# Four small moves in the queue order of an encoder-layer kernel: last dilated merge, dilated transposes, local output, q,k squares

## The chip, the cores and the metric

The kernel runs on one core of one Trainium2 chip. The metric is the device time of one execution in microseconds. Three runs of the kernel before gave 1829.3, 1828.5 and 1827.25 us, median 1828.5.

## What is computed

One encoder layer on x of 1024 tokens by 1024 features, float32:

```
x += 1/2 * post(SwiGLU_1(pre(x)))
qkv = pre(x) @ w_qkv                       # 16 heads of 64
o_na  = neighbourhood_attention(heads 0-7)     # 16 x 64 token grid, window 8 x 16, learned bias
o_dil = softmax-weighted mixture over (window, dilation) in (128,1), (512,4), (2048,16), heads 8-15
x += post(concat(rmsnorm(o_na), rmsnorm(o_dil)) @ w_out)
x += 1/2 * post(SwiGLU_2(pre(x)))
```

Each `pre` and `post` is an RMS norm with a gain. For the dilated heads each pattern gives an output and a log-sum; the outputs are merged with the softmax of the log-sums.

## The kernel before, in words

**Matmuls.** Products are made in float32r with two parts for each operand: a high part (a cast, on ScalarE) and a low part (the operand minus its high part, on VectorE), and three matmuls high*high, high*low, low*high. A 128x512 block of output is one PSUM bank. The large products (feed-forward, q,k,v) use seven-product block schemes; the output projection is plain.

**Order.** The program is written out by hand for TensorE: within the `ordered()` blocks its instructions run as written. The other engines' queues are put in order by the framework's scheduler, from the written order and its own idea of when an operation is ready, except where `c.behind(f, engine...)` ties all that f issues behind the last instruction written so far for that engine. Two queues of small work are carried along with the matmuls. `c.todo` holds turns: one entry is taken at each `c.tick()`. `c.steps` and `c.sums` hold smaller pieces: `c.step()` takes one of each. `plan(n, {turn: [...]})` fills `c.todo`, after first running everything that is left.

**Value and q,k start.** `Passes.run(0, 1)` for the value projection has 12 turns, of one `c.step()` each for the first eight and two for the last four. During them the last four 128-token tiles of x are finished: `Finish.rest(ts, h)` puts on `c.sums` two additions (L892), then `Operand.norm` (L218): the squares on ScalarE (L166), tied behind what was written last for ScalarE, after which the root (`rstd_of`, L147 to L159, a chain of twelve or thirteen small VectorE operations) and the scaling of the tiles (L230) follow as further entries. `A(4, 5)` and `A(6, 7)` are such calls for tiles 4, 5 and 6, 7; their x is loaded before. `U(4)` puts tile 4's transposes (L174) on `c.steps`, and `pg.split_left(0)` makes the parts of the first q,k weights (L462, L463), tied behind VectorE's and ScalarE's last. Then `pg.ahead` starts q,k: matmuls at L472, L473 (high part of the weight) and L478 (low part). `pg.save` copies an accumulator out (L488) before more is added to it.

**Attention.** Heads 8 to 15 (dilated) come first, then heads 0 to 7 (neighbourhood). A unit is one pair of score blocks: scores into PSUM (L1192, L1325), bias and maximum on VectorE (L1095), exponential on ScalarE (L1097), and, three units later, transposes on TensorE (L1105), the copy of them (L1107, by turns on VectorE and ScalarE), and one unit later the product with v (L1225, L1341). Every second unit ends with `c.tick()`, so a turn is two units. For each pair of dilated heads one pattern's outputs go through HBM to be regrouped (L1251 is the load back), and `DilPair.merge` makes the weights: small VectorE operations L1261 to L1271 with one exponential between (L1264), then two products on GpSimd (L1281, L1282) and the addition on VectorE (L1285). Merge, products, nothing, addition take a turn each. Only the last pair (head pair 7) has `self.then`, which is `attended()`: it queues the norm of the dilated outputs, first four turns of squares (L1370), the root and the first scaling, an empty turn, four turns with transposes, casts and low parts (`GroupNorm.put`, L174, L181), then `begin`, which makes the 16 fillers (the output projection's matmuls that only need the first half of the dilated rows), then the second half in the same way. Fillers are placed between later units at a rate of 16 / (units left + 2); what is left over comes behind the last unit.

**Local output.** After the last unit, TensorE runs the first half of a product that needs only dilated rows into four held banks (L363 to L365), and between its matmuls it transposes the eight 128-token blocks of the local heads' output (`GroupNorm.put` with `strip`, L1401; two PSUM buffers, so a block waits for the block before the last to be read). Each block has two halves, each a cast (L1405) and a low part (L1406). The first four blocks share one root and the last four another (`early[1].scale`, root and two scalings, L1390); the latter's own squares of the last head are made on VectorE (L1378).

Of the kernel before, what the change touches and what calls it, by code (L numbers as in the profile page):

```python
# [10 lines left out]
F32 = mybir.dt.float32  # L11
# [5 lines left out]
SP, POOL, DVE, ACT = [getattr(mybir.EngineType, e) for e in ("SP", "Pool", "DVE", "Activation")]  # L17
# [160 lines left out]
def transpose_in(c, x, hi, lo):  # L178

    ps = transposed(c, x)  # L180
    c.nc.scalar.copy(hi, ps)  # L181
    c.nc.vector.tensor_sub(lo, ps, hi.bitcast(F32))  # L182
    return ps


class Operand:
# [58 lines left out]
    def put(self, t):  # L245

        for i in range(2):
            self.c.steps.append(lambda: self.one(t))
# [862 lines left out]
class DilPair:  # L1111
# [97 lines left out]
    def outs(self, hd, part, quad, un, pt, po):  # L1209
        c, nc = self.c, self.c.nc  # L1210
        if un == 0:
            po.append(c.pso.tile([P, 4, P], F32, tag="o", name="po"))
        po, f = po[0], slice(hd * 64, hd * 64 + 64)
        if (part, quad, un) == (0, 1, 0):
            nc.tensor.matmul(po[:, 0:4:3, f], pt[:, 1, :], self.va[:, 8:10, f], start=True, stop=False,
                             skip_group_check=True)
            for j in range(2):
                nc.tensor.matmul(po[:, 3 * j, f], pt[:, 2 * j, :], self.va[:, 7 + 3 * j, f], start=False, stop=True,
                                 skip_group_check=True)
        else:  # L1220
            for j, blk in enumerate(self.blocks(part, quad, un)):
                o = 1 + j if quad and not part else un * 2 + j
                for t in range(2):
                    rhs = self.vb[:, blk // 2, t, :] if part else self.va[:, blk - 1 + t, :]
                    nc.tensor.matmul(po[:, o], pt[:, 2 * j + t, :], rhs, start=t == 0, stop=t == 1)  # L1225
        if un == 0:
            return
        to = self.oa.rearrange("p (a b) w -> p a b w", a=2)[:, :, 0:4:3, f] if quad else (
            self.oa.rearrange("p (a b) w -> p a b w", a=2)[:, :, 1:3, f])
        got = po[:, :, f]  # L1230
        if part:
            to = self.ob.rearrange("p (j c) w -> p c j w", j=2)[:, 2 * quad:2 * quad + 2, :, f]
            got = got.rearrange("p (c j) w -> p c j w", j=2)
        else:
            got = got.rearrange("p (a b) w -> p a b w", a=2)
        (nc.scalar.copy if quad else nc.vector.tensor_copy)(to, got)
        if hd and part:
            self.regroup(quad)
        c.tick()
        if (hd, part, quad) == (1, 0, 1):  # L1240
            c.todo.extend([lambda: None] + [lambda: c.behind(self.merge, DVE, ACT)])

    def regroup(self, quad):

# [10 lines left out]
    def merge(self):  # L1255

        c, nc, sa, obn = self.c, self.c.nc, self.sa, self.obn
        w = c.op.tile([P, 2, 8, 2], F32, tag="w", name="w")
        mn = c.op.tile([P, 8, 2], F32, tag="mn", name="mn")
        na, nb = sa[:, :, 0:2], obn[:, :, P:P + 2]  # L1260
        nc.vector.tensor_tensor(mn, na, nb, op=ALU.min)  # L1261
        nc.vector.tensor_sub(w[:, 0], mn, na)
        nc.vector.tensor_sub(w[:, 1], mn, nb)
        nc.scalar.activation(w, w, AF.Exp)  # L1264
        dn = c.op.tile([P, 2, 8, 2], F32, tag="dn", name="dn")
        nc.vector.tensor_mul(dn[:, 0], w[:, 0], sa[:, :, 2:4])
        nc.vector.tensor_mul(dn[:, 1], w[:, 1], obn[:, :, P + 2:P + 4])
        nc.vector.tensor_add(dn[:, 0], dn[:, 0], dn[:, 1])
        nc.vector.reciprocal(dn[:, 0], dn[:, 0])
        nc.vector.tensor_mul(w[:, 0], w[:, 0], dn[:, 0])  # L1270
        nc.vector.tensor_mul(w[:, 1], w[:, 1], dn[:, 0])  # L1271

        def bc(i):
            return w[:, i].unsqueeze(3).broadcast_to([P, 8, 2, 64])

        def hv(a):
            return a.rearrange("p b (h f) -> p b h f", h=2)
        a4, b4 = hv(self.oa), hv(obn[:, :, 0:P])

        def products():  # L1280
            nc.gpsimd.tensor_mul(b4, b4, bc(1))  # L1281
            nc.gpsimd.tensor_mul(a4, a4, bc(0))  # L1282

        def add():
            nc.vector.tensor_add(hv(c.og[1][:, :, self.pi * P:(self.pi + 1) * P]), a4, b4)  # L1285
        c.todo.extendleft(([self.then] if self.then else []) + [lambda: c.behind(add, DVE), lambda: None,
                          lambda: c.behind(products, POOL)] + ([] if self.then else [lambda: None]))


def na_v(c, p):  # L1290
# [65 lines left out]
class GroupNorm:  # L1356
# [35 lines left out]
    def put(self, i):  # L1392
        c, nc, b, ot = self.c, self.c.nc, self.b0 + i, self.ot
        o = self.og[:, b, :]
        if not self.strip:
            hi, lo = [ot[b // 4][:, j, :, b % 4 * P:b % 4 * P + P] for j in range(2)]
            transpose_in(c, o, hi, lo)
            return
        ps = c.pst.tile([P, 4, P], F32, tag="tr", name="trp")
        for j in range(4):  # L1400
            nc.tensor.transpose(ps[:, j, :], o[:, j * P:(j + 1) * P], c.ident)  # L1401
        for hf in range(2):
            src = ps[:, :, hf * 64:hf * 64 + 64].rearrange("p k (r c) -> p k r c", r=8)
            hi, lo = [ot[hf][:, j].rearrange("p k (r s c) -> p k r s c", r=8, s=8)[:, :, :, b, :] for j in range(2)]
            nc.scalar.copy(hi, src)  # L1405
            nc.vector.tensor_sub(lo, src, hi.bitcast(F32))  # L1406


def layer(tc, a, out):
    nc = tc.nc  # L1410
    c = Ctx(tc)
    with ExitStack() as ctx:
# [51 lines left out]
        def plan(n, at):  # L1464

            c.flush()

            def turn(fs):
                return lambda: [f() for f in fs]
            c.todo.extend(turn(at.get(i, ())) for i in range(n))  # L1470
# [146 lines left out]
        def queued(f):  # L1617

            c.behind(f, SP, POOL)
# [6 lines left out]
        with ExitStack() as order:  # L1626
# [140 lines left out]
            A = lambda *ts: lambda: fin.rest(ts, hs.get)  # L1767

            def vearly(p, t, ps):
# [4 lines left out]
                else:  # L1774
# [3 lines left out]
            pg = PairGemm(c, op, [(a["wqk"][p], a["wqk"][8 + p]) for p in QK_ORDER], 8, QKPairs(c))  # L1778
# [2 lines left out]
            vp.fetch([[w1[:, 0:2], w1[:, 2:4]]])  # L1781
            op.tied = True
            plan(12, {0: [lambda: fin.scale(4, 4), A(4, 5)], 8: [op.second, lambda: c.steps.append(lambda: None), U(4), lambda: queued(pg.start)],
                      9: [lambda: c.behind(lambda: pg.split_left(0), DVE, ACT)], 10: [A(6, 7)]})
            vp.run(0, 1, upto=1)
            e.close()
            early_pools(e, 2, 2)
# [74 lines left out]
        def attended():  # L1862

            ops.close()
            c.xt = pool("xt2", 1, s1)
            xo["part"] = pool("hs0", 1, s1).tile([P, 4, D], F32, name="hs")
            ot = xo["dil"] = [c.xt.tile([P, 2, 4, T], F32R, tag=f"o{h}", name=f"o{h}") for h in range(2)]
            norms = [GroupNorm(c, og[1], b, xo["gd"][:, 512:], False, ot, False) for b in (0, 4)]
            puts = [lambda i=i, n=n: (i < 3 and n.scaled(i + 1), n.put(i)) for n in norms for i in range(4)]
            squares = [lambda i=i: c.behind(lambda: norms[1].squares(slice(0, 512), 0, (i, i + 1)), ACT) for i in (0, 2)]  # L1870
            single = [lambda i=i: c.behind(lambda: norms[0].squares(slice(0, 512), 0, (i,)), ACT) for i in range(4)]
            scales = [lambda n=n: c.behind(lambda: n.scale(1), DVE) for n in norms]

            def begin():
                xo["ws"] = nat_fillers(c, ot[0], xo["part"], (1, 0))
                c.rate = len(c.fillers) / (c.left + 2)
            c.todo.extend(single + [scales[0], lambda: None] + puts[:4] + [begin] + squares + [scales[1], lambda: None])
            c.todo.extend(puts[4:])

        def last(quad):  # L1880
# [6 lines left out]
        early = []  # L1887
# [8 lines left out]
        with ordered():  # L1896
# [31 lines left out]
            puts = deque()  # L1928
            for quad, n in enumerate(early):
                n.ot = on  # L1930
                for i in range(4):
                    if quad and i < 2:
                        puts.append(lambda i=i, n=n: (c.behind(lambda: n.scaled(i + 2), DVE), n.put(i)))
                    elif not quad and i == 0:
                        puts.append(lambda n=n: (n.put(0), c.behind(lambda: early[1].scale(2), DVE)))
                    else:
                        puts.append(lambda i=i, n=n: n.put(i))
        s5.close()
# [3 lines left out]
        with ordered():  # L1942
# [18 lines left out]
            pg = gate_pairs(3, op, a["wg2"], a["wu2"], 11)  # L1961
# [3 lines left out]
            A = lambda *ts: lambda: fin.rest(ts, lambda t: hs[t // 4][:, t % 4, :])  # L1965
# [90 lines left out]
```

## Time and profile before

| | us |
|---|---|
| median of three runs | 1828.5 |
| the profiled execution | 1826.53 |
| its span, first to last instruction | 1824.7 |
| TensorE busy | 1807.9 |
| VectorE busy | 1308.9 |
| ScalarE busy | 831.6 |
| GpSimd busy | 348.8 |

The granted TensorE clock was 0.999 over the span. In rows of the timeline the columns are the start in us from the span's start, the duration in us, the engine (PE TensorE, DVE VectorE, ACT ScalarE, POOL GpSimd, SP SyncE), the source line where the view has one, the operation, the output and input tiles with their shapes, and in brackets the idle time of that engine before it with what ended it. "L" and a number is a line of the kernel before.

### The profile page before, as it was taken

To read this page: it belongs to the slowest core of one execution; us is meant where nothing else is said; L and a number is where in the kernel's file an instruction comes from. 1 tells how busy PE (TensorE), PEld (TensorE's weight loads), DVE (VectorE), ACT (ScalarE), POOL (GpSimd) and SP (SyncE) were. 2 spreads that over 40 slices of the span, in tenths; PEclk is the share of its full clock that TensorE was granted. 3 is DMA by queue.
4 is the path that set the end of the run, shared out by engine and by line. 5 is a ranking of instruction groups with operands and counts; after the bars stand their busy time and mean duration, and the time that the engine had idled before them with its cause. 6 is when DMAs were issued, how large, how long until landed. Compare 5 with 4: busy or idle time off the path is not lost. (4 is left out here: it accounts for less than half of the span.)

```text
span 1824.7 us, 25161 instructions
## 1 busy us (share of the span) xinstructions
PE 1807.9 (99%) x8876; PEld 1521.7 (83%) x8876; DVE 1308.9 (72%) x2225; ACT 831.6 (46%) x1495; POOL 348.8 (19%) x579
## 2 busy tenths in 40 slices
PE   8999999999999999999999999999999999999998
PEld 6888888888888888888999998887888888888886
DVE  6888877776466877577676856778877777664557
ACT  7522233334534556234688765554223333354433
POOL 2124421112021123232344100221111111110000
PEclk9999999999999999999999999999999999999999
DMA  8756566557888867768687523594655566596564
GB/s 295 258 170 220 171 230 224 193 209 268 307 305 294 288 206 266 261 230 292 193 271 255 183 88 116 193 312 159 197 180 194 201 220 224 184 351 198 191 229 146
DMA packets 172769, 409.28 MB, mean 224 GB/s; under 512 B 20401, under 2 KB 42321, under 8 KB 170594
## 3 DMA queue, kind: packets, MB, share of 16 engines
q1 hardware_dynamic: 125168, 248.68, 41.5%
q0 software_dynamic: 46608, 157.41, 23.7%
q8 instruction: 70, 1.15, 0.3%
q10 hardware_dynamic: 866, 1.58, 0.2%
q14 instruction: 57, 0.47, 0.1%
HBM read 280.09 MB, written 132.56 MB: 226 GB/s over the span
## 5 line engine op out<-in xcount | busy, mean ns | idle before, releaser
L472 PE MATMUL mmp<-x,whi 128*128 128x512 f32 (+1 forms) x1464 | 571.7, 391 | 1.1 <-ACT x L181 0.7
L473 PE MATMUL mmp<-x,whi 128*128 128x512 f32 (+1 forms) x1464 | 569.1, 389 | 0.7 <-DVE x L182 0.7
L793 PE MATMUL accp<-pw 128*128 128x512 f32 x1800 | 411.1, 390 | 0.0
L793 PEld LDWEIGHTS accp<-pw 128*128 128x128 f32 x1800 | 337.2, 188 | 70.0 <-ACT hb L814 0.3
L478 PE MATMUL mmp<-x,wlo 128*128 128x512 f32 (+1 forms) x1464 | 390.5, 388 | 0.2 <-DVE wlo L463 0.2
L472 PEld LDWEIGHTS mmp<-x,whi 128*128 128x128 f32 x1464 | 275.7, 188 | 58.7 <-ACT s L488 1.4
L473 PEld LDWEIGHTS mmp<-x,whi 128*128 128x128 f32 x1464 | 275.7, 188 | 57.2 <-DVE x L182 1.4
L478 PEld LDWEIGHTS mmp<-x,wlo 128*128 128x128 f32 x1464 | 274.4, 188 | 57.4 <-DVE wlo L463 0.6
L761 DVE TENSOR_TENSOR pw<-praw,pw 128x1024 fp32r<-128x1024 f32 (+1 forms) x181 | 200.1, 1143 | 125.6 <-ACT pw L760 124.8
L760 ACT CAST pw<-praw 128x1024 fp32r<-128x1024 f32 (+1 forms) x181 | 168.7, 983 | 207.7 <-PE accp L793 167.3
L462 ACT CAST whi<-wraw 128x1024 fp32r<-128x1024 f32 x126 | 132.6, 1053 | 187.4 <-PE mmp L473 157.9
L463 DVE TENSOR_TENSOR wlo<-wraw,whi 128x1024 fp32r<-128x1024 f32 x126 | 153.9, 1222 | 2.9 <-ACT whi L462 2.9
L703 POOL DMA_DIRECT2D g<-sg x44 | 23.9, 544 | 427.6 <-DVE sg L696 246.5
L462 ACT CAST whi<-traw 128x512 fp32r<-128x512 f32 x52 | 32.3, 621 | 122.6 <-DVE traw L564 89.7
L488 ACT COPY s<-mmp 128x512 f32<-128x512 f32 x49 | 28.8, 588 | 127.7 <-PE mmp L478 121.1
L655 DVE TENSOR_TENSOR c<-mmp,u 128x512 f32<-128x512 f32 x52 | 35.9, 691 | 70.9 <-PE mmp L478 70.7
L563 DVE TENSOR_TENSOR wraw<-wraw 128x1024 f32<-128x1024 f32 x52 | 63.6, 1224 | 17.7 <-DMA wraw<-in_wu_dram 17.0
L793 PE MATMUL accp<-pw,x 128*128 128x512 f32 x312 | 71.8, 390 | 0.0
L1095 DVE CUSTOM_DVE_ANT_0 s<-sp,g 128x256 f32<-128x256 f32 (+1 forms) x128 | 48.4, 413 | 30.7 <-PE sp L1192 24.6
L793 PEld LDWEIGHTS accp<-pw,x 128*128 128x128 f32 x312 | 58.3, 188 | 12.4 <-DVE pw L761 0.3
L642 DVE TENSOR_TENSOR c<-mmp,v 128x512 f32<-128x512 f32 x52 | 35.8, 689 | 34.0 <-PE mmp L478 34.0
L1341 PE MATMUL po<-vs,pt 128*128 128x128 f32 x352 | 49.9, 276 | 0.4 <-DVE pt L1107 0.4
(281 smaller groups left out, 2485.7 us busy)
## 6 DMA issues: line engine op xcount, KB each, us to landing
praw<-g SPq DMA_DIRECT2D x70, 512.0 KB
wraw<-in_wg_dram SPq DMA_DIRECT2D x44, 512.0 KB
wraw<-in_wu_dram SPq DMA_DIRECT2D x44, 512.0 KB
tr<-in_wd_dram SPq DMA_DIRECT2D x44, 512.0 KB
g<-sg POOLq DMA_DIRECT2D x88, 256.0 KB, 5.4
ts<-tr POOLq DMA_DIRECT2D x22, 1024.0 KB, 4.7
praw<-ts SPq DMA_DIRECT2D x88, 256.0 KB
praw<-in_wd_dram SPq DMA_DIRECT2D x66, 256.0 KB
```

The lines of the kernel that those rows point to most:

```text
L462: nc.scalar.copy(hi, raw)
L463: nc.vector.tensor_sub(lo, raw, hi.bitcast(F32))
L472: mm(out, hi[:, i, sl], xhi[:, k, cols], start=not go_on and k == 0, stop=False, skip_group_check=go_on)
L473: mm(out, hi[:, i, sl], xlo[:, k, cols], start=False, stop=False, skip_group_check=go_on)
L478: mm(out, lo[:, i, sl], xhi[:, k, cols], start=False, stop=k == 3, skip_group_check=go_on)
L563: nc.vector.tensor_sub(r[:, 0:2], r[:, 1:3], r[:, 0:2])
L655: c.behind(lambda: nc.vector.tensor_add(c21, d, u2), *((DVE,) if self.sink.soon and b == self.n - 1 else ()))
L760: nc.scalar.copy(hi, raw[:, :m])
L761: nc.vector.tensor_sub(lo, raw[:, :m], hi.bitcast(F32))
L793: c.nc.tensor.matmul(acc[t], a, b, start=not chained and gi == 0 and j == i == 0, stop=end and j + n >= len(ops) and i == len(two) - 1, sk ...
L1095: c.nc.vector.tensor_tensor_reduce(out=s, in0=ps, in1=bias, scale=-1.0, scalar=3e38, op0=ALU.add, op1=ALU.min, accum_out=neg)
L1341: nc.tensor.matmul(po[0][:, u], pt[0][:, j, :], vs[:, k0 + j, :], start=j == 0, stop=j == n - 1)
```

## The change

No operation is added or removed. Five places change the order in which work is queued:

- The merge of the last pair gets a second empty turn ahead of it. `self.then` is called in the turn of the addition, no longer in a turn of its own; for the other pairs nothing changes.
- In `attended()` a second empty turn stands between the first root and the first transposes of the dilated rows; all that follows there moves a turn later.
- In `GroupNorm.put` with `strip`, both casts are issued ahead of both low parts.
- The second root of the local output (with its first two scalings) is queued behind the last VectorE instruction before the first block, no longer behind the first block's low parts.
- `A(6, 7)` moves from turn 10 to turn 7 of the 12.

```diff
-            c.todo.extend([lambda: None] + [lambda: c.behind(self.merge, DVE, ACT)])
+            c.todo.extend([lambda: None] * (2 if self.then else 1) + [lambda: c.behind(self.merge, DVE, ACT)])
...
-        c.todo.extendleft(([self.then] if self.then else []) + [lambda: c.behind(add, DVE), lambda: None,
-                          lambda: c.behind(products, POOL)] + ([] if self.then else [lambda: None]))
+
+        def added():
+            c.behind(add, DVE)
+            if self.then:
+                self.then()
+        c.todo.extendleft([added, lambda: None, lambda: c.behind(products, POOL)] +
+                          ([] if self.then else [lambda: None]))
...
+        lows = []
         for hf in range(2):
...
             nc.scalar.copy(hi, src)
-            nc.vector.tensor_sub(lo, src, hi.bitcast(F32))
+            lows.append((lo, src, hi.bitcast(F32)))
+        for args in lows:
+            nc.vector.tensor_sub(*args)
...
-                      9: [lambda: c.behind(lambda: pg.split_left(0), DVE, ACT)], 10: [A(6, 7)]})
+                      9: [lambda: c.behind(lambda: pg.split_left(0), DVE, ACT)], 7: [A(6, 7)]})
...
-            c.todo.extend(single + [scales[0], lambda: None] + puts[:4] + [begin] + squares + [scales[1], lambda: None])
+            c.todo.extend(single + [scales[0], lambda: None, lambda: None] + puts[:4] + [begin] + squares + [scales[1], lambda: None])
...
-                        puts.append(lambda n=n: (n.put(0), c.behind(lambda: early[1].scale(2), DVE)))
+                        puts.append(lambda n=n: (c.behind(lambda: early[1].scale(2), DVE), n.put(0)))
```

## Prediction

> **What bounds the kernel now.** I read the page first, then the busy time of each engine in the three stretches that the change touches, then the timelines of TensorE, VectorE and ScalarE around every gap there.
>
> ```profile
> span 1824.7 us, 25161 instructions
> ...
> PE 1807.9 (99%) x8876; PEld 1521.7 (83%) x8876; DVE 1308.9 (72%) x2225; ACT 831.6 (46%) x1495; POOL 348.8 (19%) x579
> ```
>
> TensorE is busy for 99% of the span, so an edit that adds and removes no matmul can win only what TensorE waits. The next rows give, for the q,k start, the last dilated merge and the local output, the length, then the busy time of PE, PEld, DVE, ACT and POOL with instruction counts, the granted clock, the DMA share and the GB/s.
>
> ```profile
> 655.00:690.00 35.00, 34.88 (x162) 28.59 (x161) 30.86 (x67) 23.67 (x40) 11.72 (x21) 1.00 0.77 257
> 1003.00:1040.00 37.00, 36.19 (x294) 34.71 (x294) 29.57 (x110) 27.18 (x83) 5.40 (x5) 1.00 0.47 164
> 1095.00:1126.00 31.00, 30.40 (x180) 25.58 (x180) 22.31 (x74) 16.48 (x52) 2.37 (x5) 1.00 0.15 46
> ```
>
> Here TensorE idles 35.00 - 34.88 = 0.12, 37.00 - 36.19 = 0.81 and 31.00 - 30.40 = 0.60 us, 1.53 us in all. That is too low a cap, because a matmul counts as busy until its modelled end, after the next one could have begun. The loss is better read from the starts: how much later the next matmul starts than after the same work without a wait. VectorE is busy for 30.86 of 35 us at the q,k start; that matters below.
>
> **The last merge, one turn later.** A turn is two attention units. The first operation of the merge stands in VectorE's queue before the regrouped outputs have landed, and a softmax is queued behind it:
>
> ```profile
> 1009.48 0.18 DVE L1261 TENSOR_TENSOR mn<-sa,obn 128x16 f32<-128x16 f32 x1 [0.95 <-DMA obn<-rg]
> ```
>
> TensorE then waits for a transposed probability tile that VectorE copies too late:
>
> ```profile
> 1010.85 0.38 PE L1105 MATMUL ptp<-ident,pb 128*128 128x128 f32 x2
> 1011.63 0.94 PE L1341 MATMUL po<-vs,pt 128*128 128x128 f32 x6 [0.40 <-DVE pt L1107]
> 1012.32 0.60 PE L1325 MATMUL sp<-st 128*128 128x384 f32 x2
> 1012.76 0.38 PE L1105 MATMUL ptp<-ident,pb 128*128 128x128 f32 x2
> 1012.98 0.61 PE L1341 MATMUL po<-vs,pt 128*128 128x128 f32 x4
> ```
>
> From two transposes to the next product it is 11.63 - 10.85 = 0.78 us here and 12.98 - 12.76 = 0.22 us a unit later: 0.56 us lost. From 10.85 to 12.76 one unit takes 1.91 us, 1.35 without the loss, so a turn is 2.7 us. That covers the 0.95 us wait for the DMA by 1.7 us. The merge's ten small operations come as before, and the 1.55 us that they and the wait cost together (0.95 and about 0.6 of small operations ahead of the late copy) made 0.56 us of loss, so the pipeline absorbs about 1.0; the 0.6 alone are hidden. Gain 0.56 us; if the landing were as late again, nothing.
>
> The rest of the merge moves with it, except the call that begins the norm: it now comes in the turn of the addition instead of one turn later, so its squares stay where they were.
>
> ```profile
> 1012.66 1.90 POOL L1282 TENSOR_TENSOR oa<-oa,w 128x1024 f32<-128x1024 f32 x1 [16.05 <-DVE w L1271]
> 1014.53 1.90 POOL L1281 TENSOR_TENSOR obn<-obn,w 128x1024 f32<-128x1024 f32 x1
> ```
>
> ```profile
> 1016.46 1.23 DVE L1285 TENSOR_TENSOR og<-oa,obn 128x1024 f32<-128x1024 f32 x1 [0.30 <-POOL obn L1281]
> ```
>
> The merge's first operation could have issued at 9.48 - 0.95 = 8.53; a turn later is 11.2, or 1.8 us after its present place. The two products follow and would end at about 1016.4 + 1.8 = 1018.2. The addition's place, 16.46 - 0.30 - 0.56 + 2.7 = 1018.3, is just behind it: a wait of 0 to 0.5 us on VectorE, of the size of the 0.30 that costs nothing now. I take 0. The squares would wait on ScalarE only if the addition ended after their turn, two turns behind the old addition (16.16 - 0.56 + 5.4 = 1021.0); it ends at 1018.3 + 1.23 = 1019.5, so 1.5 us cover it.
>
> **The dilated transposes, one turn later.** The chain of small operations for the root of the norm is interleaved with softmaxes and ends late:
>
> ```profile
> 1035.51 0.83 PE L1341 MATMUL po<-vs,pt 128*128 128x128 f32 x6
> 1036.77 0.63 PE L174 MATMUL trp<-ident,og 128*128 128x128 f32 x4 [0.42 <-DVE og L1390]
> ```
>
> Six products and their follower are 1.26 us apart here and 12.32 - 11.63 = 0.69 us above: 0.57 us lost. With 2.7 us more the rows are scaled long before, so 0.57 us is gained. What moves along are four transposes, their casts and low parts, the first filler of the output product, the second half's squares and scaling. The 16 fillers stay the same matmuls, but are paced over 26 instead of 28 counted units (0.615 instead of 0.571 a unit): TensorE's sum is the same, and a denser filler gives VectorE more time per unit. The turns end before the last head's first turn, so nothing runs out: 0, at worst one more wait of the size seen here, 0.5 us.
>
> **Local output: casts ahead of low parts.** Each transposed block has two halves; ScalarE casts a half, VectorE subtracts it from the same PSUM tile.
>
> ```profile
> 1111.25 0.37 ACT L1405 CAST n<-trp 128x256 fp32r<-128x256 f32 x1 [3.32 <-PE trp L1401]
> 1112.85 0.65 ACT L1405 CAST n<-trp 128x256 fp32r<-128x256 f32 x2 [1.23 <-DVE n L1406]
> ```
>
> ```profile
> 1112.40 0.42 DVE L1406 TENSOR_TENSOR n<-trp,n 128x256 fp32r<-128x256 f32 x1
> 1113.25 0.42 DVE L1406 TENSOR_TENSOR n<-trp,n 128x256 fp32r<-128x256 f32 x1 [0.44 <-ACT n L1405]
> 1113.60 0.15 DVE L147 TENSOR_TENSOR v<-gss 128x4 f32<-128x4 f32 x1
> ```
>
> ```profile
> 1113.12 0.39 PE L364 MATMUL accp<-wlo,o 128*128 128x512 f32 x1
> 1113.34 0.40 PE L365 MATMUL accp<-whi,o 128*128 128x512 f32 x1
> 1113.82 0.63 PE L1401 MATMUL trp<-ident,og 128*128 128x128 f32 x4
> ```
>
> The second cast starts at 1112.85, when the first low part has ended (1112.40 + 0.42), though it doesn't read its result. So the first block gives its buffer back at 1113.67, and the third block's transposes, which take that buffer, start 0.48 us after the matmul before instead of 0.22 to 0.23: 0.25 us lost. With both casts first, they run at 1111.25 and about 1111.6, the low parts follow back to back at 1112.40 and 1112.75, and the buffer is free at 1113.17, 0.4 us ahead of TensorE's 1113.57. Gain 0.25 us, at least 0.
>
> [...]
>
> **Local output: second root sooner.** The second half's root stands behind the first block's low parts, from 1113.60, and its scaled rows come late for the fifth block:
>
> ```profile
> 1117.31 1.42 DVE L1390 SCALAR_TENSOR_TENSOR og<-og,y,gd 128x512 f32<-128x512 f32 x2
> ```
>
> ```profile
> 1117.39 0.39 PE L365 MATMUL accp<-whi,o 128*128 128x512 f32 x1
> 1118.21 0.63 PE L1401 MATMUL trp<-ident,og 128*128 128x128 f32 x4 [0.43 <-DVE og L1390]
> ```
>
> 0.82 instead of 0.23 us: 0.59 lost. The root needs 17.31 - 13.60 = 3.71 us with the low parts that slip in between. Queued before the first block it can start at about 1112.5, behind the last local squares. The first scaled row is then there at 1112.5 + 3.71 + 0.75 = 1117.0, TensorE at 1117.39 + 0.23 - 0.25 = 1117.37. Gain 0.59 us with 0.4 to spare; one more low part in the chain (0.42) and little of the spare is left, so 0.2 to 0.59.
>
> **Squares of q,k's last two tiles.** Their additions, squares and root are queued three turns sooner, before the fifth tile's transposes and the first weights' split instead of after all of it. No load moves, since both tiles are already on the chip. Now the squares hold up ScalarE (two of 1.06 us, the second here), behind them the copy that releases the first q,k accumulator:
>
> ```profile
> 681.62 1.06 ACT L166 ACTIVATE junk<-x 128x1024 bf16<-128x1024 f32 x1
> ```
>
> ```profile
> 683.14 0.59 ACT L488 COPY s<-mmp 128x512 f32<-128x512 f32 x1
> ```
>
> ```profile
> 680.77 0.60 PE L174 MATMUL trp<-ident,x 128*128 128x128 f32 x4
> 681.12 0.48 PE L472 MATMUL mmp<-x,whi 128*128 128x512 f32 x1
> ...
> 682.14 1.08 PE L478 MATMUL mmp<-x,wlo 128*128 128x512 f32 x4
> 683.06 0.60 PE L174 MATMUL trp<-ident,x 128*128 128x128 f32 x4
> 683.78 0.50 PE L472 MATMUL mmp<-x,whi 128*128 128x512 f32 x1
> ```
>
> The matmul at 683.78 starts as that copy ends (683.73), 0.72 us after the transposes, against 0.35 at 680.77: 0.37 lost, and gained back. The squares' new place is ScalarE's pause ahead of this copy:
>
> ```profile
> 674.08 0.59 ACT L1771 COPY vt<-accp 128x512 f32<-128x512 f32 x1 [2.10 <-DMA vs<-vt]
> ```
>
> But their root and one scaling now fall into VectorE's densest stretch, ahead of the low parts of the first two weight pairs:
>
> ```profile
> 679.80 1.22 DVE L463 TENSOR_TENSOR wlo<-graw,whi 128x1024 fp32r<-128x1024 f32 x1
> ```
>
> ```profile
> 687.63 1.28 DVE L230 SCALAR_TENSOR_TENSOR x<-x,y,gain 128x1024 f32<-128x1024 f32 x1
> ```
>
> The second low part ends at 681.02 and is read at 682.14: 1.1 us to spare. In front of it come 1.28 us of scaling and twelve small operations, an estimated 0.1 us each where they overlap with longer ones (0.15 in the row at 1113.60), 2.4 us together, less an estimated 0.6 of pauses (VectorE's 4.1 us of idle time in these 35, over 5 us): 1.8 - 1.1 = 0.7 us of new wait, if the queue keeps the program's order; 0 if that low part is issued first; 1.4 if the first weight pair is late too. I take 0.4. Together about 0: between -0.37 and +1.0.
>
> **Sum.** -0.56 - 0.57 - 0.25 - 0.59 - 0.37 + 0.4 = -1.9 us. The profiled execution took 1826.53 us (span 1824.7 and 1.8 around it), 2.0 below the median of 1828.5; from it the change gives 1824.6, on the median 1826.6, or 0.1%. A difference under 0.2% (3.7 us) is about what can't be told from no change here.
>
> **The rivals.** (a) Everything works and q,k adds no wait; each stall also slowed the matmuls just behind it (six products take 0.94 us after the wait at 1011.63, 0.83 at 1035.51: 0.1 a stall, 0.3 for three): -0.56 - 0.57 - 0.25 - 0.59 - 0.37 - 0.3 = -2.6, so 1825.9. For it: each gain has its own row and its cover. Against it: the full VectorE at q,k.
> (b) The gains are given back: VectorE at q,k costs the full +1.0 net of the 0.37, and half of the other 1.97 returns as a late softmax or weight split: 0.0, so 1828.5. For it: VectorE at 30.86 of 35 us. Against it: 29.57 of 37 and 22.31 of 31 in the other two stretches leave room.
> (c) Slower: the root and its two scalings go as one block ahead of the first low parts of the local output, because they now stand earlier in the program. That is 3.71 less six low parts that now slip in (6 x 0.34 = 2.0), so 1.7, or up to 2.6 at 0.2 us a step, and 1.42 for the scalings: about 4.0. The first block's buffer comes free at 1113.17 + 4.0 = 1117.2 instead of before 1113.57: 3.6 us of wait, which replaces the 0.84 of the local output. Net -0.56 - 0.57 + 0.03 + 3.6 = +2.5, so 1831.0. It costs anything from 0.4 us of such a block on, and makes the kernel slower from about 1.5 on. Against it: in the present queue low parts do slip between the steps of the root, at 1113.25 before and, by the pitch of 3.71 us for 1.7 to 2.6 us of steps, during it.
> (d) The casts' reorder or the earlier root does nothing, as their queue order is set by other ties: -1.9 + 0.84 = -1.1, so 1827.4.
>
> **How the numbers follow.** The forecast as summed 0.50, (a) 0.20, (b) 0.12, (c) 0.05, (d) 0.13. None of them is faster by 3.7 us; (c) reaches +2.5. What is left beyond the bound is measurement (the three runs lie 2 us apart) and a reordering of queues elsewhere that no row shows: 0.06 faster, 0.06 slower, 0.88 within. The range goes from 1824.3, (a) less 1.6 for the spread of the runs, to 1829.2, (b) and 0.7 of spread; (c) lies outside.
>
> **What would show it.** Right: no wait on the DMA before the merge's first operation, and 0.2 us from the transposes to the product there; transposes 0.2 us behind their predecessor at the dilated rows and at the third and fifth local block; two casts in a row on ScalarE for each local block. Wrong: a wait for a weight's low part at 679 to 684 of over 1 us; low parts at the local output behind the whole root; a total idle time in the last two stretches that is not below 0.81 and 0.60.

## The result and the profile after

Measured side by side with the kernel before (21 runs of each), the changed kernel takes 1831.67 us (1829.55 to 1835.96) against 1826.86 us (1824.28 to 1831.25): a ratio of 1.0025, 95% interval 1.0019 to 1.0031, so slower by about 4.6 us. The forecast was 1826.6 and "same"; the result lies above the range, where rival (c) stood. Lines of the kernel after are up to 8 higher: the local output's transposes, casts, low parts and scalings are L1406, L1411, L1414 and L1395, the product with v L1346, the transposed tile's copy still L1107.

The page of the profiled execution after: span and busy times.

```profile
span 1831.1 us, 25162 instructions
...
PE 1810.1 (99%) x8876; PEld 1525.3 (83%) x8876; DVE 1310.9 (72%) x2225; ACT 832.9 (45%) x1495; POOL 349.4 (19%) x579
```

The span grew by 6.4 us with the same 8876 matmuls, yet TensorE's busy time grew by 2.2. So part of the loss is idle time, and part is matmuls that took longer. The same three stretches as before (length, busy PE, PEld, DVE, ACT and POOL, granted clock, DMA share, GB/s):

```profile
655.00:690.00 35.00, 33.94 (x158) 27.73 (x157) 31.15 (x68) 22.84 (x41) 11.87 (x21) 1.00 0.74 243
1003.00:1040.00 37.00, 36.75 (x300) 35.48 (x300) 29.46 (x111) 27.45 (x81) 4.88 (x4) 1.00 0.57 192
1095.00:1126.00 31.00, 27.35 (x155) 23.74 (x155) 20.74 (x70) 16.17 (x49) 0.00 (x0) 0.89 0.11 35
```

TensorE's idle time went from 0.12 to 1.06 us at the q,k start, from 0.81 to 0.25 at the dilated merge, and from 0.60 to 3.65 at the local output, where the granted clock fell to 0.89 too. Three readings follow, the largest first.

**Local output.** TensorE's timeline after, from the last matmul ahead of the third block's transposes:

```profile
1116.17 0.40 PE L365 MATMUL accp<-whi,o 128*128 128x512 f32 x1
1120.21 1.09 PE L1406 MATMUL trp<-ident,og 128*128 128x128 f32 x4 [3.65 <-DVE n L1414]
1120.95 0.78 PE L363 MATMUL accp<-whi,o 128*128 128x512 f32 x1
1121.53 0.63 PE L364 MATMUL accp<-wlo,o 128*128 128x512 f32 x1
1121.95 0.63 PE L365 MATMUL accp<-whi,o 128*128 128x512 f32 x1
...
1126.50 0.39 PE L365 MATMUL accp<-whi,o 128*128 128x512 f32 x1
```

VectorE in the same time, the root from its first step to its last, then the two scalings and the first two blocks' low parts:

```profile
1115.40 0.16 DVE L147 TENSOR_TENSOR v<-gss 128x4 f32<-128x4 f32 x1
...
1117.79 0.16 DVE L159 SCALAR_TENSOR_TENSOR y<-e,y 128x4 f32<-128x4 f32 x1
1117.98 1.42 DVE L1395 SCALAR_TENSOR_TENSOR og<-og,y,gd 128x512 f32<-128x512 f32 x2
1119.31 1.42 DVE L1414 TENSOR_TENSOR n<-trp,n 128x256 fp32r<-128x256 f32 x4
```

and ScalarE, the casts of the first two blocks:

```profile
1114.07 0.65 ACT L1411 CAST n<-trp 128x256 fp32r<-128x256 f32 x2 [3.32 <-PE trp L1406]
1115.21 0.65 ACT L1411 CAST n<-trp 128x256 fp32r<-128x256 f32 x2 [0.49 <-PE trp L1406]
```

The first block's casts are done at 1114.72, and its buffer waits only for its low parts. These stand behind an unbroken root (1117.98 - 1115.40 = 2.58 us) and two scalings (1119.31 - 1117.98 = 1.33). The third block's transposes start 4.04 us after the matmul before them instead of 0.23: 3.8 us lost. Then something that the prediction did not price: the 512-wide matmuls come every 0.42 us (1121.53 to 1121.95) instead of 0.23. The granted clock, in stretches of 1 us, says why:

```profile
1118.00:1119.00 1.00, 0.00 (x0) 0.00 (x0) 1.00 (x2) 0.00 (x0) 0.00 (x0) 1.00 0.00 0
1119.00:1120.00 1.00, 0.00 (x0) 0.00 (x0) 1.00 (x4) 0.00 (x0) 0.00 (x0) 0.74 0.00 0
1120.00:1121.00 1.00, 0.79 (x5) 0.82 (x5) 0.73 (x3) 0.00 (x0) 0.00 (x0) 0.50 0.00 0
...
1126.00:1127.00 1.00, 1.00 (x6) 0.77 (x6) 0.00 (x0) 0.00 (x0) 0.00 (x0) 0.85 0.00 0
```

The clock was halved while TensorE waited and stayed so long after. In slices of 0.1 us it is 1.00 up to 1119.40, 0.88 in the slice to 1119.50 and 0.50 from there on. A mean of 0.74 then means half speed for 0.26 / 0.5 = 0.52 of that microsecond, so from 1119.48; 0.85 means 0.30, so until 1126.30. From 1120.21 to 1126.30 TensorE worked 6.1 us at half speed, which loses 3.0. The local output lost 3.8 + 3.0 = 6.8 us here, in place of the 0.84 that it lost before. The 3.0 is more than most executions pay. Each execution has its mean clock on record, to three digits; 6.8 us at half speed take 0.0019 off it, 3.4 us 0.0009. This execution has 0.997, as one other of the 21; sixteen have 0.998 and three 0.999. So this is a rough count, but about 1.5 us is the likelier clock loss of the median execution.

**q,k start.** TensorE, then VectorE:

```profile
682.56 0.40 PE L473 MATMUL mmp<-x,whi 128*128 128x512 f32 x1
684.02 1.19 PE L478 MATMUL mmp<-x,wlo 128*128 128x512 f32 x4 [1.06 <-DVE wlo L463]
```

```profile
679.14 1.28 DVE L230 SCALAR_TENSOR_TENSOR x<-x,y,gain 128x1024 f32<-128x1024 f32 x1
680.33 2.50 DVE L305 TENSOR_TENSOR x<-s,x 128x512 fp32r<-128x512 f32 x4
682.74 1.22 DVE L463 TENSOR_TENSOR wlo<-graw,whi 128x1024 fp32r<-128x1024 f32 x1
```

The second low part ends at 683.96 and not at 681.02 as before, 2.9 us later. Of that, 0.65 is no delay: TensorE reaches the whole stretch later in this execution (its first L472 starts at 677.79 instead of 677.14). It is 2.3 us later against TensorE, which loses 684.02 - 682.56 - 0.23 = 1.23 us by it. The 0.37 at the first accumulator's copy is gone.

**Dilated merge and transposes.** The last merge's first operation follows without a wait, and both old stalls are gone. Two smaller ones stand behind the move, of 0.41 and 0.27 us by the starts:

```profile
1014.34 0.17 DVE L1261 TENSOR_TENSOR mn<-sa,obn 128x16 f32<-128x16 f32 x1
```

```profile
1026.50 0.71 PE L1346 MATMUL po<-vs,pt 128*128 128x128 f32 x4 [0.25 <-ACT pt L1107]
...
1040.58 0.94 PE L1346 MATMUL po<-vs,pt 128*128 128x128 f32 x6
```

**And one loss that the change doesn't touch.** The merge of the third pair waited for its regrouped outputs in this execution, which cost TensorE 1.36 us:

```profile
987.30 0.18 DVE L1261 TENSOR_TENSOR mn<-sa,obn 128x16 f32<-128x16 f32 x1 [2.37 <-DMA obn<-rg]
```

```profile
988.62 0.60 PE L1225 MATMUL po<-va,pt 128*128 128x128 f32 x3 [1.20 <-ACT pt L1107]
```

That this comes and goes by execution, other traces show: the wait in front of this merge is 1.94 us in experiment 5, which has neither the squares nor the root moved, and absent in experiment 1, which has all but the root.

The account by starts: +6.8 - 0.8 (local output), +1.2 - 0.4 (q,k), -0.6 - 0.6 + 0.4 + 0.3 (dilated), +1.4 (third pair) makes +7.7; the two spans differ by 6.4, and the rest are differences elsewhere that no row here accounts for. Without the third pair, and with 1.5 for the clock instead of 3.0, it makes +4.8; the medians differ by 4.8. So close a match is partly luck, as each term is read from one execution.

### The profile page after: what moved, and what is told of

It is laid out like the page before. It is cut to its first block, busy times and chain, and to the rows that moved or that the text cites. A ratio compares the mean times of both kernels' runs of the same rounds, so it can differ in the third digit from the quotient of the medians.

```text
span 1831.1 us, 25162 instructions
## 1 busy us (share of the span) xinstructions
PE 1810.1 (99%) x8876; PEld 1525.3 (83%) x8876; DVE 1310.9 (72%) x2225; ACT 832.9 (45%) x1495; POOL 349.4 (19%) x579
## 5 line engine op out<-in xcount | busy, mean ns | idle before, releaser
L472 PE MATMUL mmp<-x,whi 128*128 128x512 f32 (+1 forms) x1464 | 571.4, 390 | 0.7 <-ACT x L181 0.7
L472 PEld LDWEIGHTS mmp<-x,whi 128*128 128x128 f32 x1464 | 275.7, 188 | 57.1 <-ACT x L181 1.3
L1346 PE MATMUL po<-vs,pt 128*128 128x128 f32 x352 | 50.0, 276 | 0.4 <-ACT pt L1107 0.2
```

The lines of the kernel that those rows point to most:

```text
L472: mm(out, hi[:, i, sl], xhi[:, k, cols], start=not go_on and k == 0, stop=False, skip_group_check=go_on)
L1346: nc.tensor.matmul(po[0][:, u], pt[0][:, j, :], vs[:, k0 + j, :], start=j == 0, stop=j == n - 1)
```

## The experiments

My theory after the result: the root with its scalings, as one block ahead of the first low parts, causes the whole slow-down, and the halved clock is part of its price; the other four moves together gain a little. The rivals: the q,k squares cause as much of it, or the moves do harm only together. All ratios are to the kernel before on the same chip, in five rounds; experiments 1 to 4, 5 to 8 and 9 ran on three different chips, on which the kernel before took 1826.89, 1827.62 and 1826.55 us.

**1. Root back.** The changed kernel, with the second root behind the first block's low parts again.

```diff
-                        puts.append(lambda n=n: (c.behind(lambda: early[1].scale(2), DVE), n.put(0)))
+                        puts.append(lambda n=n: (n.put(0), c.behind(lambda: early[1].scale(2), DVE)))
```

> The changed kernel with the second local root behind the first block's low parts again; merge, dilated transposes, casts ahead and the earlier squares stay. Theory A (the root and its two scalings stand as one block ahead of the low parts, and the 3.65 us of idle time also halve the matmul pitch for some 6 us behind it): the wait of 3.8 us at the third block and the slow matmuls (about 2.4 us) are gone, a wait of at most 0.6 us at the fifth block is back; about 5.5 us less than the changed kernel, near 1826.3, within 0.1% of before. Theory B (the later merge and the denser fillers cost the time): little changes, 1830 to 1832.

1825.95 us against 1826.89, ratio 0.9995 (0.9986 to 1.0004). So this one line turns +0.25% into no difference: 1.0025 - 0.9995 is 5.5 us, where the two traces, one execution each, show 6.8 and 0.35 us lost at the local output. VectorE's order shows what the line decides:

```profile
1113.78 0.75 DVE L1414 TENSOR_TENSOR n<-trp,n 128x256 fp32r<-128x256 f32 x2
1114.44 0.15 DVE L147 TENSOR_TENSOR v<-gss 128x4 f32<-128x4 f32 x1
...
1114.91 0.42 DVE L1414 TENSOR_TENSOR n<-trp,n 128x256 fp32r<-128x256 f32 x1
```

```profile
1118.95 0.63 PE L1406 MATMUL trp<-ident,og 128*128 128x128 f32 x4 [0.18 <-DVE og L1395]
```

The first block's two low parts go first, then root steps with the later blocks' low parts between them; only the fifth block is 0.35 us late.

**2. Root alone.** The kernel before with only that line changed.

```diff
-                        puts.append(lambda n=n: (n.put(0), c.behind(lambda: early[1].scale(2), DVE)))
+                        puts.append(lambda n=n: (c.behind(lambda: early[1].scale(2), DVE), n.put(0)))
```

> The kernel before with only the second local root queued ahead of the first block. Theory A: the low part of the first half of the first block comes behind the twelve steps of the root, that of the second half behind the scalings too, so TensorE waits over 4 us at the third block, and about 0.43 instead of 0.23 us lie between matmul starts behind it: +5 to +6.5 us, near 1832.5. Theory B: no loss, 1826 to 1827.

1831.2 us, ratio 1.0026 (1.0016 to 1.0035): the slow-down needs no other part. It is 4.7 us by the ratio, a little less than the 5 to 6.5 expected. TensorE's timeline, then the stretches of 1 us around its wait:

```profile
1118.83 1.09 PE L1401 MATMUL trp<-ident,og 128*128 128x128 f32 x4 [3.52 <-DVE n L1406]
```

```profile
1118.00:1119.00 1.00, 0.17 (x1) 0.21 (x2) 1.00 (x3) 0.00 (x0) 0.00 (x0) 0.83 0.00 0
1119.00:1120.00 1.00, 1.00 (x5) 1.00 (x5) 0.43 (x2) 0.42 (x2) 0.00 (x0) 0.50 0.00 0
...
1122.00:1123.00 1.00, 1.00 (x6) 0.83 (x5) 0.42 (x1) 0.43 (x2) 0.00 (x0) 0.96 0.00 0
```

Half speed from 1118.66 (0.17 / 0.5 = 0.34) to 1122.08: 3.42 us, half as long as in the changed kernel's trace, and 1.6 us lost.

The recorded mean clocks of all executions say the same without any trace. Where the root stands ahead of the first block (the changed kernel, experiments 2, 7 and 9), 9 of 52 executions have a mean clock of 0.999, and the others 0.998 or 0.997. Where it stands behind (experiments 1, 3, 4, 5, 6 and 8), 64 of 66 have 0.999.

**3. Squares alone.** The kernel before with `A(6, 7)` at turn 7.

```diff
-                      9: [lambda: c.behind(lambda: pg.split_left(0), DVE, ACT)], 10: [A(6, 7)]})
+                      9: [lambda: c.behind(lambda: pg.split_left(0), DVE, ACT)], 7: [A(6, 7)]})
```

> The kernel before with only the additions, squares and root of tiles 6 and 7 three turns sooner. Theory A: the low part of the second q,k weight comes behind the scaling of tile 6 and four low parts, one wait of about 1.2 us near 684, the 0.37 us of before gone: +0.9 us, near 1827.8. Rival: the wait at 684 in the changed kernel came from other moves, so this one gains 0.3 us: 1826.5.

1828.11 us, ratio 1.0007 (0.9997 to 1.0016): not told from nothing, on the slow side. Two low parts are late here, 0.35 and 1.42 us by the starts:

```profile
680.16 1.21 PE L478 MATMUL mmp<-x,wlo 128*128 128x512 f32 x4 [0.19 <-DVE wlo L463]
...
684.90 1.19 PE L478 MATMUL mmp<-x,wlo 128*128 128x512 f32 x4 [1.25 <-DVE wlo L463]
```

In all five traces with the squares sooner and their root with them, the second low part cost 1.04 to 1.43 us, and in two of them the first about 0.4 more.

**4. Merge and transposes.** The kernel before with the first two parts of the change.

```diff
-            c.todo.extend([lambda: None] + [lambda: c.behind(self.merge, DVE, ACT)])
+            c.todo.extend([lambda: None] * (2 if self.then else 1) + [lambda: c.behind(self.merge, DVE, ACT)])
...
+        def added():
+            c.behind(add, DVE)
+            if self.then:
+                self.then()
...
-            c.todo.extend(single + [scales[0], lambda: None] + puts[:4] + [begin] + squares + [scales[1], lambda: None])
+            c.todo.extend(single + [scales[0], lambda: None, lambda: None] + puts[:4] + [begin] + squares + [scales[1], lambda: None])
```

> The kernel before with only the last merge and the dilated transposes a turn later. Theory A: the two waits of 0.56 and 0.57 us go, -1.1 us, near 1825.7. Theory B: new waits in the dilated heads (1.2 us in the changed kernel's profile, ahead of the third pair's merge) come from this part, +0.5 to +2 us, 1827.5 to 1829. If those waits are the landing of a transfer that differs between executions, they are neither always here nor never in before.

1825.59 us, ratio 0.9991 (0.9983 to 1.0000): at the edge of a gain, 1.6 us by the point estimate. What the later merge avoids depends on the execution. In the kernel of experiment 2, whose merge is the old one, TensorE waited nearly four times as long at that place as in the profile before (0.40); in experiments 3 and 6, whose merge is the old one too, it waited 1.1 and 1.2 us.

```profile
1013.20 0.60 PE L1341 MATMUL po<-vs,pt 128*128 128x128 f32 x3 [1.52 <-DVE pt L1107]
```

**5. Merge, transposes and casts.** Experiment 4 and the reordered casts.

```diff
+        lows = []
         for hf in range(2):
...
             nc.scalar.copy(hi, src)
-            nc.vector.tensor_sub(lo, src, hi.bitcast(F32))
+            lows.append((lo, src, hi.bitcast(F32)))
+        for args in lows:
+            nc.vector.tensor_sub(*args)
```

> The kernel before with the later merge, the later dilated transposes and the casts ahead of the low parts, without the earlier root and the earlier squares. Theory A: -1.1 us from the first two and -0.25 to -0.6 from the casts (third, fourth and sixth to eighth local blocks start without a wait, the root starts 0.4 us sooner by itself): near 1825.3. Rival: the cast order does nothing, 1825.7.

1824.19 us against 1827.62, ratio 0.9984 (0.9975 to 0.9993): faster. The stretches:

```profile
1003.00:1040.00 37.00, 36.64 (x298) 35.17 (x298) 29.87 (x111) 27.51 (x82) 5.09 (x5) 1.00 0.51 177
1095.00:1126.00 31.00, 30.80 (x188) 26.61 (x187) 22.45 (x75) 17.03 (x53) 2.60 (x5) 1.00 0.14 47
```

Idle time is 0.36 and 0.20 us, against 0.81 and 0.60 before.

**6. Casts alone.** The kernel before with the diff of experiment 5 only.

> The kernel before with only the casts ahead of the low parts. Theory A: two casts in a row on ScalarE for each block, the wait of 0.25 us at the third local block gone, the 0.59 us at the fifth reduced or unchanged: -0.3 to -0.6 us, near 1826.4, not to be told from before by the time, but by the starts in the profile. Rival: the second cast still waits for VectorE, and the starts are as before.

1826.12 us, ratio 0.9993 (0.9985 to 1.0002): not resolved alone. Its trace has no late third block, and the fifth loses 0.37 instead of 0.59. It also answers a question of the q,k start, where its work is that of the kernel before:

```profile
683.74 0.60 PE L174 MATMUL trp<-ident,x 128*128 128x128 f32 x4
684.25 0.50 PE L472 MATMUL mmp<-x,whi 128*128 128x512 f32 x1
```

From the transposes to the matmul it is 0.51 us here, 0.72 in the profile before, 1.05 in the trace of experiment 2 and 0.44 in that of experiment 5, with 0.35 where nothing is late. The 0.37 that the squares' move should win back was one draw out of 0.1 to 0.7.

**7. One scaling behind.** The changed kernel with the root and one scaling ahead of the first block, the other scaling behind it.

```diff
-                        puts.append(lambda n=n: (c.behind(lambda: early[1].scale(2), DVE), n.put(0)))
+                        puts.append(lambda n=n: (c.behind(lambda: early[1].scale(1), DVE), n.put(0), c.behind(lambda: early[1].scaled(1), DVE)))
```

> The changed kernel with one of the two scalings moved behind the first block's low parts, so that the wait at the third local block falls from 3.65 to about 3.0 us of idle time; nothing else differs. If the slow matmuls behind the wait need an idle time of over 3.0 us: 0.7 us of wait and about 2.4 us of slow matmuls go, 3.1 us less than the changed kernel, near 1828.6. If an idle time of 3.0 us slows them as well, or they are slow for another reason: 0.7 us less, near 1831.

1830.11 us, ratio 1.0014 (1.0005 to 1.0022). Counted from the changed kernel's 1.0025, 3.1 us less would be 1.0008 and 0.7 us less 1.0021; the time lies between and does not decide. The profile does. The wait fell by 0.67 us, one scaling, so the block's length does set it:

```profile
1118.69 1.09 PE L1406 MATMUL trp<-ident,og 128*128 128x128 f32 x4 [2.98 <-DVE n L1414]
```

```profile
1118.00:1119.00 1.00, 0.31 (x2) 0.34 (x3) 1.00 (x3) 0.00 (x0) 0.00 (x0) 0.57 0.00 0
...
1121.00:1122.00 1.00, 1.00 (x7) 0.96 (x6) 0.25 (x1) 0.16 (x1) 0.00 (x0) 0.72 0.00 0
```

The clock was halved all the same, from 1118.14 to 1121.56: 3.42 us again.

**8. Squares sooner, their root late.** Experiment 5, and `A(6, 7)` at turn 7 with the root and the scalings of these tiles left at turn 11.

```diff
-        self.half, self.raw, self.tied, self.place = {}, {}, False, {}
+        self.half, self.raw, self.tied, self.place, self.later = {}, {}, False, {}, False
...
-        self.c.sums.append(lambda: self.scale(*n))
+        self.root = lambda: self.c.sums.append(lambda: self.scale(*n)); self.later or self.root()
...
-                      9: [lambda: c.behind(lambda: pg.split_left(0), DVE, ACT)], 10: [A(6, 7)]})
+                      9: [lambda: c.behind(lambda: pg.split_left(0), DVE, ACT)], 7: [lambda: setattr(op, "later", True), A(6, 7)], 11: [lambda: (setattr(op, "later", False), op.root())]})
```

> The later merge, the later dilated transposes, the casts ahead, and for tiles 6 and 7 the additions and squares three turns sooner, but the root and the scaling at their old place. Theory A: ScalarE's copy comes in time without VectorE's low part coming late, so the 0.37 us near 684 go and no 1.2 us come: 0.3 us less than the kernel without the squares' move, near 1825.0, 0.1% under before. Rival: the squares by themselves delay the cast or the copies there, 1825.5 to 1826.5.

1824.37 us, ratio 0.9980 (0.9971 to 0.9989): the fastest ratio, though not told apart from experiment 5. The stretch of the q,k start has no idle time at all:

```profile
655.00:690.00 35.00, 35.00 (x163) 28.91 (x162) 32.81 (x70) 24.38 (x42) 11.77 (x21) 1.00 0.74 254
```

So the squares themselves do no harm there; the root and the scaling that came along with them do.

**9. Root ahead, both scalings behind.** This asks when the clock is halved.

```diff
-                        puts.append(lambda n=n: (c.behind(lambda: early[1].scale(2), DVE), n.put(0)))
+                        puts.append(lambda n=n: (c.behind(lambda: early[1].scale(0), DVE), n.put(0), c.behind(lambda: [early[1].scaled(j) for j in range(2)], DVE)))
```

> The changed kernel with only the root ahead of the first local block's low parts; both scalings stand behind them. If the length of the idle time alone decides (the third block's transposes waited 3.65 us with root and both scalings ahead, 2.98 with one scaling ahead), the wait falls to 3.65 - 1.33 = 2.3 us. Theory 1, the matmuls behind a wait are slow only when the wait is long (2.4 us of extra time behind 3.65 us, about 0.8 behind 2.98): no slow matmuls behind 2.3 us, the loss at the third block is 2.3 us, and the time is about 1.3 + 2.4 = 3.7 us under the changed kernel, ratio to before about 1.0005. Theory 2, the slow matmuls come from the queue behind the wait (low parts and casts that are late too, whatever the idle time): 0.5 to 1 us of extra time remains behind the wait, ratio about 1.001.

1829.82 us against 1826.55, ratio 1.0018 (1.0009 to 1.0027). The wait is as short as foretold. Theory 1 missed: half speed came all the same. Theory 2 has a time inside the interval (1.001), but late low parts and casts do not make matmuls slow here; the granted clock does: the 512-wide ones come every 0.23 us at a clock of 1.00 (1120.10 to 1120.33) and every 0.43 at 0.50 (1122.70 to 1123.13). The half-speed stretch of this execution is as long as in the changed kernel's trace. It is the slowest of the eleven executions (1833.36 us) and the only one with a mean clock of 0.997; eight have 0.998, so most paid less.

```profile
1119.40 0.63 PE L1406 MATMUL trp<-ident,og 128*128 128x128 f32 x4 [2.20 <-DVE n L1414]
...
1121.39 1.09 PE L1406 MATMUL trp<-ident,og 128*128 128x128 f32 x4 [0.66 <-DVE n L1414]
```

```profile
1119.00:1120.00 1.00, 0.60 (x5) 0.63 (x6) 1.00 (x3) 0.00 (x0) 0.00 (x0) 1.00 0.00 0
1120.00:1121.00 1.00, 0.73 (x4) 0.25 (x2) 1.00 (x3) 0.65 (x2) 0.00 (x0) 0.82 0.00 0
...
1127.00:1128.00 1.00, 1.00 (x5) 0.77 (x5) 0.11 (x1) 0.65 (x2) 0.00 (x0) 0.77 0.00 0
```

TensorE worked at full speed from 1119.40 on and was halved at 1120.64, 1.2 us after the wait had ended, until 1127.46: 6.82 us. So half speed began here while TensorE was at work (a matmul from 1120.33 to 1120.73). What set the moment is not shown; the last section has what was measured.

## Why the prediction was wrong, point by point

**The step that failed** is the one on the second root: "Queued before the first block it can start at about 1112.5", with a root of 3.71 us "with the low parts that slip in between". It started right behind the last local squares, as foretold, and the fifth block lost its wait (1126.50 to 1126.73). But nothing slipped in: the root ran unbroken, 2.58 us, and the first block's low parts stood behind it and the scalings, so the third block started 3.8 us late. In the kernel before, the low parts between the root's steps are those of blocks whose casts come while the root runs; the first block's were already ahead of the root because the tie put them there. The move took away just that tie. VectorE's rows now have the whole root (from 1115.40) and, in the changed kernel, both scalings (from 1117.98) ahead of the first block's low parts (1119.31). I had this case as rival (c) and gave it 0.05, with the row at 1113.25 as evidence against it. That row could not speak for the new order: it showed low parts ahead of the root by a tie that the change moves. Experiments 1 and 2 show that this line alone is enough for the slow-down, and that without it there is none.

**The price of rival (c).** Its wait was right: 3.6 us foretold, 3.65 measured. (It counted six low parts between the old root's steps, where the rows have five, but its upper figure of 2.6 us for the root is what was measured.) Its sum was not: it says that the wait replaces the 0.84 lost before, yet adds the 3.6 in full. With the 0.84 taken off, the net of (c) is -0.56 - 0.57 + 0.03 + 3.6 - 0.84 = +1.7 instead of +2.5, and such a block makes the kernel slower from 2.3 us on, not 1.5. So 1831.0 came near the measured 1831.67 partly by luck. What it left out is the clock: about 1.5 us more for a half-speed stretch of 3.42 us and 3.0 for one of 6.82. With the clock, and with q,k at +0.9 instead of +0.03, (c) comes to +4.0 to +5.5, around the measured +4.8. Ahead of the halving TensorE had been idle without a break for 2.9 us in the changed kernel (1116.57 to 1119.48), 3.35 in experiment 2 and 2.4 in experiment 7, where its wait was still going on; in experiment 9 a wait of 2.20 us had ended 1.2 us before. How long a wait must be to halve the clock, these traces do not show.

**Merge, transposes and casts** went as forecast: the waits named are gone, and the casts come in pairs. Forecast -0.56 - 0.57 - 0.25 = -1.4 us; measured -0.16%, 2.9 us (1.3 to 4.6). By the point estimates, 1.6 of it is the merge and the transposes (experiment 4, 1.1 forecast) and 1.3 the casts (experiment 6, 0.25 forecast); neither is told from its forecast. The merge's share was taken from one execution, and TensorE waited longer there in the three others with the old merge, so the move spares more in those. The cover for the dilated transposes was not free: the 0.41 and 0.27 us at 1026.50 and 1040.58 are in all seven traces with these moves. The casts also eased the fifth block, from 0.59 to 0.37, which I had not counted. In the changed kernel's trace a low part waits for both casts of its block where VectorE is free. The third block's casts end at 1121.34 + 0.65 = 1121.99, and the first of its two low parts starts at 1122.02, after 1.29 us of idle time:

```profile
1121.34 0.65 ACT L1411 CAST n<-trp 128x256 fp32r<-128x256 f32 x2 [5.48 <-PE trp L1406]
```

```profile
1122.02 0.76 DVE L1414 TENSOR_TENSOR n<-trp,n 128x256 fp32r<-128x256 f32 x2 [1.29 <-ACT n L1411]
```

In the old order, in the profile before, the first block's first low part starts at 1112.40, behind its own cast (1111.25 + 0.37) and ahead of the other one (1112.85). The trace shows the wait, not its reason.

**Squares of q,k.** Mechanism right, size off. "1.8 - 1.1 = 0.7 us of new wait", of which I took 0.4, measured 1.23: against TensorE the low part came 2.3 us later and not 1.8. Of the 2.3, the scaling is 1.2, and 0.6 is one more L305: five stand ahead of the low part (677.33 and the four at 680.33) where four did before (676.79 and three at 677.39). The prediction did not count it. The remaining 0.5 are steps of the root. And the 0.37 to be gained has another size in every execution. The net was about +0.9 instead of 0.

**The sum.** Experiment 5 (-0.16%), the root alone (+0.26%) and the squares alone (+0.07%) add up to +0.17%; the whole change measured +0.25%. The rest is 1.5 us, inside the intervals. About 0.5 us of it is to be expected: the casts win 0.25 us at the third block and 0.22 at the fifth, and with the root ahead both blocks have no such wait left to win. The longer half-speed stretch of the changed kernel's trace (6.82 us, against 3.42 in that of the root alone) is not the rest by the recorded clocks: 0.997 stands on 2 of 21 executions of the changed kernel and on 2 of 9 of the root alone.

**Left open:** why the framework's scheduler interleaves the root in one case and not in the other. With the root ahead nothing slips in even though the second block's casts come while it runs (1115.21 to 1115.86). The traces show the order, not its reason.

## What to carry to other kernels

The chain that was moved ahead of a short operation delayed that operation by its whole length (TensorE waited 3.65 us with the root and both scalings ahead, 2.98 with one scaling, 2.20 with the root alone): before moving a chain, ask who waits for the short one, and take evidence from the queue's new order, since gaps in the old one belong to the old ties. Price a long wait of TensorE with the halved clock behind it: in the four traces with a wait of 2.2 to 3.65 us at the local output it was 1.4 to 3.1 us on top, by the mean clocks it was less in some executions, and a wait of 1.5 us elsewhere brought nothing (a clock of 1.00); what lies between was not measured. When a forecast says that one loss replaces another, take the old one off in the sum. And a wait for a DMA that is read from one execution is one draw: compare it over several traces before using it as a term.

## What the hardware showed that was not expected

The half-speed stretch, at a granted clock of 0.50, lasted 6.82, 3.42, 3.42 and 6.82 us in the traces of the changed kernel and experiments 2, 7 and 9. It starts at moments that no instruction marks: 0.7 us before the work resumes in the changed kernel (1119.48 and 1120.21), 1.2 us after it in experiment 9 (1120.64 and 1119.40). What sets its start and its length is not shown. At the kernel's end the clock is halved once more, when TensorE has finished; in the changed kernel, then in experiment 7:

```profile
1826.00:1827.00 1.00, 0.00 (x0) 0.00 (x0) 0.88 (x4) 0.00 (x0) 0.00 (x0) 0.52 0.00 0
```

```profile
1824.00:1825.00 1.00, 0.00 (x0) 0.00 (x0) 1.00 (x2) 0.00 (x0) 0.00 (x0) 0.85 0.00 0
```

That is at 1826.04 and 1824.70. In the changed kernel the last matmul had ended 2.2 us before, at 1823.81.

Within the half-speed stretch TensorE was idle for 0.73 and 0.66 us in the two cases of 6.82 us (changed kernel, experiment 9), and for 0.55 and 0.17 us in the two of 3.42 (experiments 7 and 2); four executions can't say whether the one goes with the other. A wait of 1.52 us (experiment 2, at 1013.20) left the clock of its stretch untouched: it was 1.00 from 1010 to 1017.
